# Sliding-window attention in a two-layer decoder kernel: queries and keys produced transposed and passed through DRAM, a query block's two score blocks merged into 128 columns, values as differences

## The chip, the cores and the metric

The kernel runs on one core of one Trainium2 chip. The metric is the device time of one execution in microseconds. Three runs before the change gave 2192.77 to 2192.95 us, median 2192.94.

The core's engines each work through an instruction queue of their own, in order: TensorE (PE in the profile; PEld is its weight load), VectorE (DVE), ScalarE (ACT), GpSimd (POOL), and SyncE (SP), which here only issues DMA transfers. They wait for each other through semaphores.

## The reference

Two layers on 1024 tokens of width 1024, batch 1. Layer 0 mixes tokens by a causal convolution module, layer 1 by sliding-window attention with 16 query heads of width 64, four groups of four heads, each group with one key and value head. After each mixer come a layer norm, a squared-ReLU MLP, another layer norm, and a gated embedding. The change concerns the attention of layer 1:

```python
q = partial_rope((x @ w_q).reshape(B, T, N_HEADS, HEAD_DIM), cos, sin)
scores = einsum("bnqkgd,bnskd->bnkgqs", q, kk) * HEAD_DIM ** -0.5
mask = (kpos >= 0) & (rel >= 0) & (rel < 128)          # rel = qpos - kpos
scores = where(mask, scores, -inf)
lse = logaddexp(logsumexp(scores, -1), sink)
out = einsum("bnkgqs,bnskd->bnqkgd", exp(scores - lse), vv)
return out.reshape(B, T, 1024) @ w_o
```

Queries come in 8 blocks n of 128 tokens; kk and vv hold for each the keys and values of the block before it and of its own, 256 positions s. A query at place a of its block sees the places s <= a of its own block and the places s > a of the block before: exactly 128 keys, one per place (block 0 sees its own only). RoPE turns the first 16 of a head's 64 dimensions.

## The kernel before

All matrices are float32, and each operand of a large product is split into a rounded high part and the rest (`split`, L533: a ScalarE cast and a VectorE subtraction; `prep`, L514, for weights). A product is then three matmuls (`mm3`, L537): high by high, high by low, low by high. One half of 512 output columns over 1024 inputs is 24 matmuls.

The program is recorded, then put in order by a scheduler (`Recorder.schedule`, L304) that keeps a cost for each operation (`cost`, L276) and writes out one fixed queue per engine; all instructions are issued from one line, L452, so the profile is read by tile names, not by lines. Tiles are slots of a tag (`SLOTS`, L51: "A" has 9, "t" 5, "z" 4, "ps" 6 banks of PSUM and so on); the requests for a tag are served in the order in which the program makes them (`serve`, L367), and `move` (L224) hands slots from one tag to another. `later` (L263) lowers the priority of what stands in it. `Stream` (L455) prepares weight units of 128x1024 in five slots ahead of use.

The order of stages is `conv`, `mlp(0)`, `ple(0)`, `attention`, `mlp(1)`, `ple(1)` (L1500 to L1506). `embed` (L853) multiplies the per-layer inputs by a projection and leaves the result in DRAM for `ple`; that of layer 1, 96 matmuls of 512 columns, stands at the end of `conv`, after layer 0's `mix_out` (L873).

In `attention` (L1307) before the change:

- For each of 8 token tiles, `tok_group` (L624) makes keys and values together: the tile's transposed input is the stationary operand, 512 weight columns move past it. `rope` (L1291) turns keys by five small operations; `split` and four TensorE transposes make them stand with dimensions on partitions, high and low part one over the other (`kT`, tag B).
- For each pair of groups `gp` and each block `n`, 24 matmuls make 512 query columns (eight heads), `rope` turns them, and GpSimd copies them doubled. Then for each of the two groups `scores` (L1397) and, one step behind, `values` (L1447) are called: 32 calls of each in all.
- `scores` transposes the queries of four heads (4 transposes), splits them, and makes two matmuls of 256 columns for each head. VectorE adds the mask, scales and takes the maximum in one operation per head; ScalarE takes the exponential of 257 columns (256 keys and the sink) and sums them in its accumulator; VectorE inverts the sum; GpSimd scales.
- `values` transposes the probabilities of four heads (4 transposes per key block, so 8), splits them, and makes 4 matmuls of 512 columns that add up in one bank; ScalarE and VectorE fold its two halves and split the result into the operand of w_o.
- `mix_out` multiplies by w_o in groups of tiles (`MIX_GROUPS`, L48): first half of the columns in two groups of four tiles, second half in four pairs, each tile followed by its layer norm.

## Time and profile before

| what | value |
|---|---|
| median of three runs | 2192.94 us |
| span of the profiled execution | 2191.9 us |
| TensorE granted clock, mean | 0.999 |
| TensorE instructions | 10395 matmuls and transposes |
| bytes moved by DMA | 303.92 MB |

In the rows of the profile an operation is named by its tiles, "written <- read", with the number of partitions and elements; "ident" as an operand marks a transpose. The attention's score banks show as "B,g", the probabilities' transposes as "ident,z", the values' products as "A,v" or "A,bo" (the tags that lent the slots). Busy time is the time in which an engine had an instruction under way; a matmul's length includes the time that its last columns need to leave the array, so back-to-back matmuls overlap in the record.

### The profile page before, as it was taken

Reading aid. Unit: us, or ns where it says so; the run is one execution under the profiler, and the core shown is the slowest. Engines: PE = TensorE matmul, PEld = TensorE weight load, DVE = VectorE, ACT = ScalarE, POOL = GpSimd, SP = SyncE. Lnnn points to the kernel's source line nnn. Section 1 sums busy time; section 2 is a strip of 40 time slices with the busy share of each in tenths; the row PEclk is TensorE's granted clock in tenths of the full one; section 3 lists DMA queues with packets and bytes.
Section 4 is the critical chain, followed back from the end, with each engine's and each line's share of the span. In section 5 each row is a group of like instructions: output and inputs, shape, how many; then the busy total and the mean of one; then the engine's idle time right before and its main releaser. Section 6 shows DMA issues by size and latency. Waiting matters only on the chain. (4 is left out here: it accounts for less than half of the span.)

```text
span 2191.9 us, 29197 instructions
## 1 busy us (share of the span) xinstructions
PE 2179.6 (99%) x10395; PEld 1813.9 (83%) x10395; DVE 1654.1 (75%) x2744; ACT 929.4 (42%) x1712; POOL 245.0 (11%) x442
## 2 busy tenths in 40 slices
PE   9999999999999999999999999999999999999999
PEld 7888878888888888888888888888888888888887
DVE  6667786967776988789644888689677689778983
ACT  4233343544443333343335878444344433333441
POOL 0000043200000000002201544240000000000040
PEclk9999999999999999999999999999999999999999
DMA  7443632534446845451431011322444496455312
GB/s 227 116 115 87 194 118 87 202 100 155 159 149 239 293 162 181 140 186 38 135 101 39 20 39 30 117 103 98 148 150 154 153 323 222 140 176 174 105 68 101
DMA packets 142914, 303.92 MB, mean 139 GB/s; under 512 B 15664, under 2 KB 43696, under 8 KB 142768
## 3 DMA queue, kind: packets, MB, share of 16 engines
q1 hardware_dynamic: 141472, 301.26, 41.9%
q8 instruction: 82, 1.34, 0.3%
q10 hardware_dynamic: 1296, 0.79, 0.1%
q14 instruction: 64, 0.52, 0.1%
HBM read 212.86 MB, written 89.13 MB: 138 GB/s over the span
## 5 line engine op out<-in xcount | busy, mean ns | idle before, releaser
L452 PE MATMUL ps<-xTh 128*128 128x512 f32 x636 | 247.4, 389 | 0.0
L452 PE MATMUL ps<-xTl,xTh 128*128 128x512 f32 x636 | 247.4, 389 | 0.0
L452 PE MATMUL ps<-xTh,xTl 128*128 128x512 f32 x636 | 247.4, 389 | 0.0
L452 PE MATMUL ps<-xTl,wh 128*128 128x512 f32 x628 | 246.6, 393 | 0.0
L452 PE MATMUL ps<-xTh,wh 128*128 128x512 f32 x628 | 245.0, 392 | 0.7 <-ACT xTh L452 0.7
L452 PE MATMUL ps<-xTh,wl 128*128 128x512 f32 x628 | 245.5, 391 | 0.0
L452 ACT CAST wh<-raw 128x1024 fp32r<-128x1024 f32 (+2 forms) x138 | 129.2, 938 | 242.3 <-PE ps L452 128.3
L452 DVE TENSOR_TENSOR wl<-raw,wh 128x1024 fp32r<-128x1024 f32 (+2 forms) x138 | 151.6, 1099 | 103.6 <-ACT wh L452 103.1
L452 PE MATMUL ps<-wh,xTh 128*128 128x512 f32 (+1 forms) x452 | 178.4, 395 | 0.3 <-ACT xTh L452 0.3
L452 PE MATMUL ps<-wl,xTh 128*128 128x512 f32 (+1 forms) x452 | 178.3, 394 | 0.0
L452 PE MATMUL ps<-wh,xTl 128*128 128x512 f32 (+1 forms) x452 | 178.2, 395 | 0.0
L452 PEld LDWEIGHTS ps<-xTh,wh 128*128 128x128 f32 x628 | 118.4, 189 | 26.2 <-ACT xTh L452 1.4
L452 PEld LDWEIGHTS ps<-xTh 128*128 128x128 f32 x636 | 119.4, 188 | 25.0
L452 PEld LDWEIGHTS ps<-xTl,xTh 128*128 128x128 f32 x636 | 119.4, 188 | 24.9
L452 PEld LDWEIGHTS ps<-xTh,xTl 128*128 128x128 f32 x636 | 119.4, 188 | 24.5
L452 PEld LDWEIGHTS ps<-xTh,wl 128*128 128x128 f32 x628 | 118.5, 189 | 24.5
L452 PEld LDWEIGHTS ps<-xTl,wh 128*128 128x128 f32 x628 | 118.5, 189 | 23.0 <-DVE xTl L452 0.2
L452 POOL TENSOR_SCALAR sm<-sm 128x1 f32<-128x1 f32 x40 | 14.6, 366 | 1056.5 <-DVE sm L452 1054.9
L452 ACT CAST xTh<-wh 128x1024 fp32r<-128x1024 f32 x74 | 77.6, 1049 | 121.9 <-PE ps L452 79.3
L452 DVE TENSOR_TENSOR wl<-g,wh 128x512 fp32r<-128x512 f32 x100 | 66.5, 687 | 81.2 <-ACT wh L452 81.2
L452 ACT CAST wh<-g 128x512 fp32r<-128x512 f32 x100 | 59.6, 620 | 159.6 <-PE ps L452 69.5
L452 DVE TENSOR_TENSOR E<-cst,g 128x1152 fp32r<-128x1152 f32 x64 | 86.1, 1353 | 43.4 <-PE ps L452 42.6
(305 smaller groups left out, 5178.2 us busy)
## 6 DMA issues: line engine op xcount, KB each, us to landing
wh<-hid SPq DMA_DIRECT2D x76, 512.0 KB, 4.2
raw<-in_w_up_dram SPq DMA_DIRECT2D x64, 512.0 KB, 3.6
wl<-in_w_down_dram SPq DMA_DIRECT2D x64, 512.0 KB, 4.6
hid<-zz SPq DMA_DIRECT2D x84, 256.0 KB, 2.9
hid<-t SPq DMA_DIRECT2D x78, 256.0 KB, 2.1
raw<-hid SPq DMA_DIRECT2D x34, 512.0 KB, 4.1
B<-scr SPq DMA_DIRECT2D x32, 256.0 KB, 4.2
t<-proj SPq DMA_DIRECT2D x32, 256.0 KB, 3.5
```

Of the source, the lines that this page charges most:

```text
L452: getattr(getattr(nc, o.eng), o.name)(*a, **k)
```

## The change

Weights of queries and keys become the stationary operand, so that the products come out with dimensions on partitions (`part_rows`); no query or key is transposed any more. The weight columns are put in order on the host so that one product of 128 rows holds the same four or eight dimensions of all heads (block 0 and 1: the two RoPE halves), and RoPE works on whole rows (`rope_queries`, `keep_keys`). High and low parts are stored to DRAM (`qd`, `kd`) and come back per block and group, gathered by head, high over low (`load_queries`, `load_keys`). The queries of the first two groups are finished before the first score, those of the other two between the halves (`rest(0)`, `rest(1)`). Values are made by a product of 256 columns per tile.

In `scores` the two key blocks' scores of a head (256 columns of a bank) are merged into 128: ScalarE copies the earlier block's, VectorE's `copy_predicated` writes the own block's over them where s <= a. Maximum and sum become `tensor_reduce` over 129 columns of four heads at once. In `values` the one merged block is transposed (4 transposes); the product uses the earlier block's values with all probabilities, and adds the difference of the two blocks' values (`load_values`) with those probabilities that belong to the own block, which GpSimd cuts out by `affine_select`. The first half's output goes through DRAM (`ad`), because its place in `xTh` and `xTl` still holds the input of `rest(1)`. Layer 1's `embed` moves from the end of `conv` to the end of the attention steps; `mix_out` of layer 1 works in pairs of tiles in both halves; tags A and B change places for layer 1's residual tiles. Of `attention`, `scores` and `values`, the diff below shows the lines after the change.

```diff
+PAIRS = ((0, 1), (2, 3), (4, 5), (6, 7))
 MIX_GROUPS = (
-    ((0, 1, 2, 3), (4, 5, 6, 7)), ((0, 1), (2, 3), (4, 5), (6, 7)),
+    (((0, 1, 2, 3), (4, 5, 6, 7)), PAIRS), (PAIRS, PAIRS),
...
-        with nc.later(EMBED_BY[1]):
-            self.embed(1, (0, 1), "t")
...
+    def part_rows(self, u, h):
+
+        wh, wl = u
+        ps = self.ps()
+        self.mm3(ps, [
+            (wh[:, kb * P : (kb + 1) * P], wl[:, kb * P : (kb + 1) * P], *self.xs(kb, h * HT, HT)) for kb in range(KB)
+        ])
+        return ps
...
+        nc.scalar.mul(h, src, HD ** -0.5)
+        nc.vector.scalar_tensor_tensor(
+            out=l, in0=src, scalar=HD ** -0.5, in1=h.bitcast(F32), op0=ALU.mult, op1=ALU.subtract
+        )
...
+    def keep_rows(self, what, pair, parts, row, first, step, h):
+
+        cols = slice(h * HT, (h + 1) * HT)
+        n = parts.stop - parts.start
+        for v, t in zip(what, pair):
+            dst = self.dram(
+                v, (row,), cols, lambda a: a[first : first + (n - 1) * step + 1 : step, cols], n
+            )
+            self.nc.sync.dma_start(dst, t.bitcast(F32)[parts])
...
+    def rope_queries(self, x1, x2, h):
+
+        nc = self.nc
+        cs, sn = (v[:, h * HT : (h + 1) * HT] for v in self.rt)
+        for k, (a, b, op) in enumerate(((x1, x2, ALU.subtract), (x2, x1, ALU.add))):
+            m, n = self.sb("t"), self.sb("t")
+            nc.vector.tensor_tensor(out=m, in0=a, in1=cs, op=ALU.mult)
+            nc.vector.tensor_tensor(out=n, in0=b, in1=sn, op=ALU.mult)
+            nc.either.tensor_tensor(out=m, in0=m, in1=n, op=op)
+            self.keep_query(m, k, 4 * k, 8, h)
...
+    def load_queries(self, n, g):
+
+        q = self.sb("X", F32R)
+        tk = slice(n * P, (n + 1) * P)
+        rows = (0, 1) + tuple(2 + 3 * (g // 2) + c for c in range(3))
+        for k, v in enumerate(self.qd):
+            src = self.dram(
+                v, rows, tk, lambda a: a.rearrange("(h r) t -> r h t", r=HD)[:, 4 * g : 4 * g + 4, tk], HD
+            )
+            dst = q.bitcast(F32)[k * HD : (k + 1) * HD].rearrange("p (h t) -> p h t", h=4)
+            self.nc.sync.dma_start(dst, src)
+        return q
...
+        self.split(src(n), v[:, :, 0, :], v[:, :, 1, :])
+        if n:
+            w = self.sb("t")[:, 0:P].rearrange("p (g e) -> p g e", g=2)
+            nc.either.tensor_tensor(out=w, in0=src(n), in1=src(n - 1), op=ALU.subtract)
+            self.split(w, d[:, :, 0, :], d[:, :, 1, :])
+        return v, d
...
+        for h in range(2):
+            ps = [self.part_rows(u, h) for u in us[2:]]
+            self.rope_queries(*ps, h)
+            for k in range(2):
+                self.keep_keys(k, self.part_rows(us[k], h), h)
+
+        def rest(s):
+            for c in range(1, 4):
+                u = ws.get(1)[0]
+                for h in range(2):
+                    self.keep_query(self.part_rows(u, h), 1 + 3 * s + c, s * HT + c, 4, h)
+                ws.done(1)
+
+        rest(0)
...
                 for gl in range(2):
+                    g = 2 * gp + gl
+                    p = self.scores(n, g, self.load_queries(n, g), keys[:, gl])
                     if pend:
                         self.values(*pend)
+                    pend = p, n, gl, gp, before, vd
+                before = vd
+            if gp == 0:
+                rest(1)
         self.values(*pend)
+        for a, b in moves:
             nc.move(b, a)
+        for q in range(4):
+            tk = slice(q * 256, (q + 1) * 256)
+            for x, v in zip((self.xTh, self.xTl), self.ad):
+                nc.sync.dma_start(x.bitcast(F32)[:, 0:4, tk], v.rearrange("p (k t) -> p k t", k=4)[:, :, tk])
+        self.embed(1, (0, 1), "t")
...
+        w = P if n == 0 else 2 * P
+        s = nc.tile("z", (P, 2 * ZC)).rearrange("p (a b) -> p a b", a=4)
+        nc.gpsimd.tensor_copy(s[:, :, P], self.sink[:, 4 * g : 4 * g + 4])
         for jj in range(2):
             ps = self.ps("sc").rearrange("p (a b) -> p a b", a=2)
             for j in range(2):
+                qs = q[:, (2 * jj + j) * P : (2 * jj + j + 1) * P]
+                nc.tensor.matmul(ps[:, j, 0:w], qs, keys[:, 0, 0:w], start=True, stop=False)
+                nc.tensor.matmul(ps[:, j, 0:w], qs, keys[:, 1, 0:w], start=False, stop=True)
+            dst = s[:, 2 * jj : 2 * jj + 2, 0:P]
+            if n == 0:
+                mask = self.mask.unsqueeze(1).to_broadcast([P, 2, P])
+                nc.vector.tensor_tensor(out=dst, in0=ps[:, :, 0:P], in1=mask, op=ALU.add)
+                continue
+            nc.scalar.copy(dst, ps[:, :, 0:P])
+            mine = self.mine.bitcast(mybir.dt.int32).unsqueeze(1).to_broadcast([P, 2, P])
+            nc.vector.copy_predicated(dst, mine, ps[:, :, P : 2 * P])
+        sm = self.small(16)
+        nm, su = (sm[:, 4 * i : 4 * i + 4] for i in range(2))
+        nc.vector.tensor_reduce(out=nm, in_=s[:, :, 0 : P + 1], axis=AXIS, op=ALU.max, negate=True)
         for h in range(4):
+            nc.scalar.activation(s[:, h, 0 : P + 1], s[:, h, 0 : P + 1], AF.Exp, bias=nm[:, h : h + 1], scale=1.0)
+        nc.vector.tensor_reduce(out=su, in_=s[:, :, 0 : P + 1], axis=AXIS, op=ALU.add)
         nc.vector.reciprocal(su, su)
         for h in range(4):
             nc.gpsimd.tensor_scalar(
+                out=s[:, h, 0:P], in0=s[:, h, 0:P], scalar1=su[:, h : h + 1], scalar2=0.0, op0=ALU.mult, op1=ALU.add
             )
+        return s
+
+    def values(self, s, n, gl, gp, before, vd):
         nc = self.nc
+        pp = self.transpose4([s[:, h, 0:P] for h in range(4)])
+        pT = [self.sb("A", F32R) for j in range(2)]
+        self.split(pp, *pT)
         po = self.ps("pv")
+
+        def v(x):
+            return x[:, gl].rearrange("p s e -> p (s e)")
+
+        tr = [(v((before or vd)[0]), p) for p in pT]
+        if n:
+            for p in pT:
+                m = self.sb("A", F32R)
+                nc.gpsimd.affine_select(
+                    out=m, in_=p, pattern=[[0, 4], [1, P]], compare_op=ALU.is_ge, fill=0.0, base=0, channel_multiplier=-1
+                )
+                tr.append((v(vd[1]), m))
         for i, (l, r) in enumerate(tr):
             nc.tensor.matmul(po, l, r, start=i == 0, stop=i == len(tr) - 1)
         pv = po.rearrange("p (a e t) -> p a e t", a=2, e=2)
             r = slice(e * HD, (e + 1) * HD)
             nc.scalar.copy(s[r], pv[0:HD, :, e, :])
             nc.vector.tensor_tensor(out=s[r], in0=s[r], in1=pv[HD:P, :, e, :], op=ALU.add)
+        g = 2 * gp + gl
+        tk = slice(n * P, (n + 1) * P)
+        if gp:
+            sl = (slice(None), slice(2 * g, 2 * g + 2), tk)
+            self.split(s, self.xTh[sl], self.xTl[sl])
+            return
+        w = self.sb("t", F32R)
+        pair = [w[:, k * 256 : (k + 1) * 256].rearrange("p (a t) -> p a t", a=2) for k in range(2)]
+        self.split(s, *pair)
+        for x, y in zip(self.ad, pair):
+            nc.sync.dma_start(x.rearrange("p (k t) -> p k t", k=4)[:, 2 * g : 2 * g + 2, tk], y.bitcast(F32))
```

More of the change, by code (lines that the diff above doesn't have):

```diff
@@ L14 @@
 ALU = mybir.AluOpType
+AXIS = mybir.AxisListType.X
 P = 128
@@ L55 @@
 LATE = 100
-EMBED_BY = (150, 0)
+EMBED_BY = 150
 MARK = (3, 3)
@@ L871, in embed, with mix_out @@
         ws.done(len(us))
-    def mix_out(self, i, w, gb, tiles, lhs=None):
+    def mix_out(self, i, w, gb, tiles):
         nc, ws = self.nc, self.ws
@@ new lines, in keep_rows, with keep_query @@
+    def keep_rows(self, what, pair, parts, row, first, step, h):
[6 more added lines that the diff above has]
+            self.nc.sync.dma_start(dst, t.bitcast(F32)[parts])
+    def keep_query(self, src, row, first, step, h):
+        pair = [self.sb("A", F32R) for k in range(2)]
+        self.scaled_split(src, *pair)
+        self.keep_rows(self.qd, pair, slice(0, P), row, first, step, h)
```

236 lines of the change are left out of this document (100 added, 136 removed).

## The prediction, made before the changed kernel was timed

> **What bounds the kernel now.** I read the page's header and part 1 first.
>
> ```profile
> span 2191.9 us, 29197 instructions
> PE 2179.6 (99%) x10395; PEld 1813.9 (83%) x10395; DVE 1654.1 (75%) x2744; ACT 929.4 (42%) x1712; POOL 245.0 (11%) x442
> ```
>
> TensorE is busy 99% of the span: work taken from it shortens the kernel as long as the rest keeps up. The windows view (length, busy time and count of PE, PEld, DVE, ACT, POOL, then granted clock, DMA share, GB/s) shows how near the others come in the stage that changes.
>
> ```profile
> 400.00:450.00 50.00, 50.00 (x225) 41.28 (x224) 49.44 (x76) 25.41 (x43) 0.29 (x1) 1.00 0.47 162
> 550.00:600.00 50.00, 50.00 (x222) 41.35 (x222) 38.34 (x59) 21.07 (x35) 0.00 (x0) 1.00 0.47 160
> 1129.90:1468.20 338.30, 337.71 (x1826) 279.97 (x1825) 243.04 (x718) 207.66 (x582) 116.66 (x254) 1.00 0.17 55
> 1200.00:1250.00 50.00, 49.93 (x303) 42.45 (x303) 41.09 (x144) 37.92 (x114) 22.43 (x60) 1.00 0.04 12
> 1250.00:1300.00 50.00, 50.00 (x291) 41.24 (x290) 44.93 (x151) 42.09 (x123) 25.55 (x61) 1.00 0.16 53
> 1400.00:1468.20 68.20, 68.20 (x320) 56.61 (x319) 44.57 (x62) 21.08 (x28) 19.44 (x21) 1.00 0.23 78
> ```
>
> Attention runs from 1129.9 (first key product) to 1468.2 (last w_o product). At 1250 TensorE is full, but VectorE is at 90% and ScalarE at 84%: the softmax steps are covered only because the query products, 12 matmuls per step, stand between them. A matmul's shown duration includes its pipeline, so I take the pace. The window at 550 holds only 512-column matmuls: 50/222 = 0.225 us each. The timeline (start, length, ...) gives the others:
>
> ```profile
> 246.74 2.56 PE L452 MATMUL ps<-B,E 128*128 128x256 f32 x20
> 1103.26 1.48 PE L452 MATMUL ps<-ident,E 128*128 128x128 f32 x12
> 1193.49 0.56 PE L452 MATMUL ps<-B,g 128*128 128x128 f32 x4
> ```
>
> Less one drain of 0.28: 0.120 us per 256-column matmul, 0.110 per transpose, 0.10 per 128-column matmul.
>
> **The change, part by part.** *TensorE.* From the order of both built programs: 400 transposes become 128 (272 x 0.110 = 29.9 us less); scores 192 of 256 columns and 96 of 128 become 224 and 32 (32.6 to 30.1 us, 2.5 less); keys and queries keep their columns, but values take 192 matmuls of 256 columns for 96 of 512 (23.0 for 21.6, 1.4 more); probabilities times values stay at 120 of 512. Sum: 31 us less work. The stage's 1826 instructions at these paces (1080 x 0.225, 192 x 0.120, 96 x 0.10, 458 transposes x 0.110) are 326 of its 338.3 us; the other 12 are small bubbles.
>
> *Where cover goes.* Now all queries of eight heads are made first, then 16 (block, group) steps follow, then the queries of the other eight heads, then 16 steps. TensorE's own work in 16 steps is 112 x 0.120 + 16 x 0.10 + 60 x 0.225 + 64 x 0.110 = 35.6 us, 2.2 a step. The order shows what is left to fill with. In the first 16 steps: 48 of the 144 matmuls of the second query half, nearly all in the first four steps; the rest, 94 in one run, comes when 15 steps are done. In the second: 46 of the 96 matmuls of the moved embedding (12 ahead, 34 among the last four steps), then 50 in one run, then w_o. Tile queues are served first come first, so the embedding's copies wait for the attention's "t" tiles, and w_o's banks for the embedding's. So the steps run at the pace of VectorE and ScalarE. Their prices, groups by form between 1180 and 1400 us (last pair: busy us, mean ns; idle behind the bar):
>
> ```profile
> L452 DVE TENSOR_TENSOR A<-ps,A 128x512 fp32r<-128x512 f32 x60 | 40.0, 686 | 5.0 <-ACT A L452 4.5
> L452 DVE TENSOR_TENSOR t<-t,ps 64x256 f32<-64x256 f32 x64 | 27.1, 424 | 7.4 <-ACT t L452 5.7
> L452 DVE CUSTOM_DVE_ANT_0 z<-ps,cst 128x256 f32<-128x256 f32 x56 | 22.8, 416 | 0.4
> L452 DVE CUSTOM_DVE_ANT_0 z<-ps,cst 128x128 f32<-128x128 f32 x8 | 2.2, 283 | 0.5 <-PE ps L452 0.3
> L452 DVE TENSOR_TENSOR xTl<-t,xTh 128x256 fp32r<-128x256 f32 x16 | 6.8, 422 | 0.6 <-ACT xTh L452 0.5
> L452 DVE RECIPROCAL sm<-sm 128x4 f32<-128x4 f32 x32 | 5.5, 172 | 4.4 <-ACT z L452 4.2
> L452 DVE TENSOR_TENSOR v<-A,v 128x128 fp32r<-128x128 f32 x5 | 1.5, 300 | 0.3 <-ACT v L452 0.3
> L452 DVE BATCH_NORM_STATS2 sm<-A 128x6 f32<-128x512 f32 x2 | 1.4, 686 | 0.0
> ...
> L452 ACT CAST A<-ps 128x512 fp32r<-128x512 f32 x60 | 33.2, 580 | 6.9 <-PE ps L452 6.9
> L452 ACT COPY t<-ps 64x256 f32<-64x256 f32 x64 | 23.3, 364 | 16.5 <-PE ps L452 9.2 <-DVE t L452 6.7
> L452 ACT CAST xTh<-t 128x256 fp32r<-128x256 f32 x16 | 6.4, 400 | 3.0 <-DVE t L452 3.0
> L452 ACT ACTIVATE z<-z,sm 128x129 f32<-128x129 f32 x16 | 6.3, 395 | 0.1
> ...
> L452 POOL COPY t<-t 128x512 f32<-128x512 f32 x32 | 20.7, 657 | 146.4 <-DVE t L452 129.5 <-issue 7.0 <-PE ps L452 4.5
> L452 POOL COPY z<-cst 128x2 f32<-128x2 f32 x60 | 15.0, 254 | 19.5 <-PE ps L452 18.2 <-PE tr L452 0.4 <-POOL z L452 0.2
> L452 POOL TENSOR_SCALAR z<-z,sm 128x128 f32<-128x128 f32 x16 | 5.7, 376 | 5.1 <-DVE sm L452 5.1
> L452 POOL TENSOR_TENSOR E<-z,g 128x512 f32<-128x512 f32 x11 | 17.8, 1628 | 12.1 <-DVE z L452 8.9 <-issue 3.2
> ```
>
> (The last row is from the whole trace.) VectorE in 16 steps: 32 masked copies or adds x 0.417 = 13.3; 32 reductions over 516 elements; 16 reciprocals 2.8; 16 splits of probabilities x 0.686 = 11.0; 32 adds x 0.424 = 13.6; 16 splits x 0.422 = 6.8; some 18 value operations x 0.30 = 5.4. A reduction isn't in the trace: from the 283 and 416 ns rows an element costs 1.04 ns, so 516 cost 0.54 us bare, and the statistics row, which reads 512 from the same memory, has 0.686; I take 0.68, that row, and keep 0.54. That is 21.8, and 75 us for 16 steps, 4.7 a step. The masked copy is bound by 0.283 (half its elements) and 0.686; it reads a bank as the 416 ns row does, so that.
>
> ScalarE: 64 exponentials x 0.395 = 25.3; 28 copies of 128x256, between 0.364 and 0.58, say 0.40, 11.2; 16 x 0.58, 32 x 0.364, 16 x 0.400 = 27.3; values 4.5: 68, and 3 to 5 for queries or embedding. GpSimd: 64 x 0.376 + 16 x 0.25 + four subtractions = 30, and 28 selections of 128x512, not in the trace: 0.657 (a copy of that shape) to 1.63 (a two-input operation), 48 to 75 us. I take 0.8, near the one-input row. On GpSimd's queue these selections stand between the scalings of the next steps, and TensorE's transposes wait for those.
>
> So 2 x 75 us of VectorE with ScalarE close behind. How full can it be? 99% at 400 us, 90% and 82% in attention before; I take 94.5%, between the first two, as here it isn't held by TensorE: 158.7 us. Each half also begins and ends with the chain through one step (a last step's split, selections and products follow VectorE's last reduction): 4 us in the first, where the run of 94 takes over early, 6 in the second. Both halves: 168.7.
>
> *Round trip.* Queries and keys go through DRAM: 220 more transfers on SP's queue (52 stores and 128 loads of queries and keys, 32 stores and 8 loads of attention output). At the start 23 us of value products hide it. Between the halves, the loads stand behind the last store on SP; that store waits for ScalarE's and VectorE's split.
>
> ```profile
> L452 SPq DMA_DIRECT2D raw<-in_w_q_dram x8: 327/332/333, 1120.3 to 1255.7; - x8
> ...
> t<-proj SPq DMA_DIRECT2D x32, 256.0 KB, 3.5
> ```
>
> 0.58 + 0.69 + two issues of 0.33 + a landing of 3.5 = 5.5 us from the last query matmul to the first score. Bounds: 0, if the 12 embedding matmuls and one step's values covered it, and twice that.
>
> *At nothing.* The embedding's 96 matmuls (21.6 us) move, and behind mix_out(0) the MLP's first products fill in, as they already do behind mix_out(1) at 1400-1468 (TensorE 68.20 of 68.20); uncovered, a normalisation's few us. Pairs in w_o's first half: weight preparation is off the path with VectorE idle there; uncovered, 2 us. RoPE on few rows, tag swaps: under the products.
>
> *Sum*, first key product to last w_o product: first products 336 x 0.225 + 23.0 + 34 leftover transposes 3.7 = 102.3; halves 168.7; 94 matmuls 21.1; round trip 5.5; 50 embedding matmuls 11.3; w_o 384 x 0.225 + 24 transposes = 89.0. Total 398; before 338.3 + 21.6 of embedding elsewhere = 359.9. **38 us more**: 31 us of TensorE work saved, some 80 of idle TensorE bought, 12 of bubbles traded. 2191.9 + 38 = 2230; the median of the runs shown, 2192.94, lies 1 us above the span: **2231**.
>
> Low end: 99% full, reductions at 0.54, half the chain ends: 2 x 70.5/0.99 + 5 = 147, 21 less: 2210. High end: 82% full: 183 + 10, 24 more: 2255.
>
> **Rivals.** (a) *The clock falls.* With 2.2 us of work in 5 TensorE may not count as busy.
>
> ```profile
> 251.62 0.47 PE L452 MATMUL ps<-wh,wh 128*128 128x512 f32 x1 [2.33 <-DVE g L452]
> ...
> 303.32 0.66 PE L452 MATMUL ps<-ident,A 128*128 128x128 f32 x4 [1.82 <-ACT t L452]
> ...
> 252.00:256.00 4.00, 4.00 (x13) 2.85 (x12) 3.02 (x5) 0.00 (x0) 0.21 (x1) 0.57 0.95 298
> ```
>
> After 2.33 us idle the granted clock fell to 0.57 of full over 4 us; after 1.82 us it didn't. A step has under 3 us idle, in several pieces, which speaks against. At half clock throughout, TensorE needs 2 x (35.6 + 48 x 0.225) = 92.8 and 2 x (35.6 + 34 x 0.225) = 86.5, and sets the pace: 179 + 10, 21 more: 2252. The Trainium skill (TensorE: Matmul & The Clock Gate, "What's actually happening") says that the clock halves after one idle window of about 3.4 us. By that rule alone the steps would keep full clock; the trace agrees in the half rate but shows that 2.33 us idle can do.
>
> (b) *GpSimd becomes the bound*, stretched as its operations are where VectorE contends: at 1.63 per selection and 0.6 per scaling (1.6 times its row) 16 steps are 90 us, /0.945 x 2 + 10 = 200, 32 more: 2263. Against: at 90% VectorE the 376 ns row held. The Trainium skill (GPSIMD Engine Reference, "Elementwise — side-by-side cycle accounting") puts data-dependent branching at about 12 cycles per element of a 1.2 GHz clock; as an estimate from that page a selection would take 5.1 us and the kernel some 190 us more. No run here shows it.
>
> (c) *Transfers bound the first half*: per step 260 KB of queries, 260 of keys, 260 of stores, in pieces of 512 B to 1 KB.
>
> ```profile
> 90.00:120.00 30.00, 30.00 (x167) 25.99 (x166) 19.18 (x29) 8.86 (x22) 0.81 (x6) 1.00 0.41 97
> ```
>
> With such pieces 97 GB/s took 0.41 of the engines, 237 GB/s full: 3.3 us a step, below 4.7. At half that rate 6.6 us, 106 + 4 for the half, 26 more: 2257.
>
> (d) *Not slower.* The halves would have to fit into 398 - 38 = 360, that is 131 us instead of 169: 60 us of VectorE for 16 steps at 99%. One mechanism can: the forms without an accumulator are cheap, reductions and masked copies at half price (75 - 17.5 = 57.5) and exponentials at 0.20 (68 - 12.5 = 56 on ScalarE): 2 x 57.5/0.99 + 10 = 126, 5 us faster: 2188. It decides from 3.7 us a step down. Against: these rows scale with elements.
>
> **How the numbers follow.** Forecast 0.62 (2231, own range 2210 to 2255); (a) 0.12; (b) 0.10; (c) 0.08; (d) 0.08. The range 2210 to 2263 leaves out (d) and a tenth of the rest. A measurement of this kernel can tell 0.2% (4.4 us) from no change: (d) splits into 0.06 faster and 0.02 the same; slower has 0.92.
>
> **What would show it.** Right: the changed profile has two stretches of some 83 us with VectorE over 85% busy, in which TensorE starts about half of what it could (drains raise its busy share), a run of query products between them with VectorE nearly idle, idle of PE ended by POOL, DVE and ACT tiles, and 272 transposes fewer. The reductions, masked copies and selections then have rows of their own. Wrong: TensorE above 90% through attention, a step under 4 us, or a stall outside attention.

## The result, and the profile after

The changed kernel takes 2252.2 us (median of 4 runs, 2249.9 to 2252.8) beside 2192.9 for the kernel before (4 runs): 1.027 of its time, 95% interval 1.025 to 1.028. The profiled execution has a span of 2250.3 us, 58.4 more than before. The direction and the range of the prediction held; its middle was 21 us too low.

The changed kernel's page: span, busy time of each engine, and two rows of the 40 slices.

```profile
span 2250.3 us, 28661 instructions
PE 2190.7 (97%) x10187; PEld 1804.0 (80%) x10187; DVE 1651.6 (73%) x2478; ACT 891.4 (40%) x1552; POOL 244.7 (11%) x431
...
PE   9999999999999999999999777999999999999999
...
PEclk9999999999999999999999879999999999999999
```

TensorE lost 208 instructions (272 transposes and 32 score matmuls less, 96 value matmuls more), and yet three slices now show it at 70 to 80% busy, where no slice of its row did before. Its total busy time even rose, by 11 us. Outside attention, where TensorE is full, it takes some 12 us longer (below). In attention its busy time fell by only 2 us (357.30, for 337.71 before and 21.6 of embedding), because shown durations are longer there at the lower clock: a score matmul of 256 columns shows 0.340 us between 1217 and 1416, before the change 0.284 and 0.307. Counts, not busy shares, tell the work here.

The windows view of the changed kernel cuts attention at its own boundaries: the whole stage; the first 16 steps and 35 us from their middle; the query products of the second half; the gap to its first score; the second 16 steps; w_o. Columns as in the prediction.

```profile
1114.10:1520.20 406.10, 357.30 (x1713) 289.57 (x1712) 243.33 (x459) 181.92 (x442) 115.89 (x245) 0.93 0.50 147
1217.80:1298.40 80.60, 63.21 (x296) 48.92 (x296) 69.53 (x156) 58.84 (x167) 44.81 (x109) 0.84 0.55 151
1245.00:1280.00 35.00, 25.78 (x118) 18.88 (x118) 31.70 (x73) 26.59 (x80) 22.29 (x54) 0.90 0.44 124
1298.40:1321.10 22.70, 22.70 (x95) 18.10 (x94) 4.87 (x8) 3.86 (x7) 0.00 (x0) 0.96 0.50 158
1321.10:1339.70 18.60, 4.22 (x20) 3.12 (x18) 5.39 (x11) 4.15 (x10) 1.46 (x3) 0.67 1.09 292
1339.70:1416.10 76.40, 60.21 (x286) 46.81 (x287) 65.92 (x151) 57.67 (x169) 45.35 (x109) 0.88 0.42 109
1428.50:1520.20 91.70, 91.70 (x420) 75.52 (x419) 52.17 (x71) 24.73 (x33) 19.44 (x21) 1.00 0.24 82
```

Attention took 406.1 us; before it took 338.3, and the embedding that has moved into it some 21.6 elsewhere: 46 us more. The first steps are as forecast in kind: in the middle of a half VectorE is at 91% (31.70 of 35) while TensorE starts 118 instructions in 35 us, 3.4 a us, where before it started 5.8 a us (x291 in 50). Only the first 21 us of the first half are different: there the query products that the order left among the first steps keep TensorE full (21.20 of 21.20 us up to 1239). Between the halves VectorE nearly idles (4.87 of 22.70). Then comes what was forecast at 5.5 us and took 18.6. The stage began at 1114.1, where 1129.9 - 21.6 = 1108.3 was due, and 730.1 us followed it, where 723.7 did before: another 12 us (5.8 + 6.4) lie outside attention.

The same kernel's waits of TensorE between 1327 and 1416 (total, times, longest), the chain to the first score from the split of the query product that block 0 waits for, the last for tokens 0 to 511 (start, length, what), and two rows of SyncE's queue in that stretch:

```profile
PE ps L454 <- DMA X<-qdl: 14.4, 1, 14.4
PE tr L454 <- DVE t L454: 5.2, 7, 1.4
PE ps L454 <- POOL z L454: 4.5, 5, 1.8
```

```profile
1315.79 0.61 ACT A L454
...
1316.41 8.75 DMA qdh<-A
...
1327.88 5.65 DMA X<-qdh
...
1333.55 6.12 DMA X<-qdl
...
1339.71 4.78 PE ps L454 x20
```

```profile
1325.23 5.41 SPq L454 DMA_DIRECT2D X<-qdh  x8
...
1333.55 6.32 SPq L454 DMA_DIRECT2D X<-qdl  x8
```

The store of the high parts took 8.75 us to land and the first two loads 5.65 and 6.12, under a DMA share of 1.09 (the row of 1321.10 above). The second load could not have gone out much earlier even if the first had landed sooner: on SyncE's queue the high parts of eight steps and four other transfers are issued ahead of the first low part, from 1325.23 to 1333.55, 8.3 us in all with no pause over 0.5 us. The DMA issues of that stretch (1300 to 1345; KB each, median us to landing) name what else was under way:

```profile
xTl<-adl SPq DMA_DIRECT2D x4, 512.0 KB, 8.1
xTh<-adh SPq DMA_DIRECT2D x4, 512.0 KB, 6.4
X<-qdh SPq DMA_DIRECT2D x10, 128.0 KB, 5.6
...
X<-qdl SPq DMA_DIRECT2D x8, 128.0 KB, 6.3
```

The reload of the first half's attention output is eight transfers of 512 KB, 4 MB in all. Six of them are issued between 1312.7 and 1318.9, each as soon as the last query products have read the place that it fills, and so they are under way together with the query stores and loads for which TensorE waits.

The prices that the prediction had to bound, from the changed kernel's groups by form between 1217 and 1416:

```profile
L454 ACT ACTIVATE z<-z,sm 128x129 f32<-128x129 f32 x128 | 47.7, 403 | 18.3 <-DVE sm L454 17.4
L454 POOL TENSOR_SCALAR z<-z,sm 128x128 f32<-128x128 f32 x128 | 47.5, 384 | 116.4 <-DVE sm L454 88.8 <-ACT z L454 27.2 <-ACT v L454 0.5
L454 DVE TENSOR_REDUCE sm<-z 128x4 f32<-128x516 f32 x64 | 43.5, 682 | 1.9 <-ACT z L454 0.8
L454 POOL TENSOR_SCALAR_AFFINE_SELECT A<-A 128x512 fp32r<-128x512 f32 x56 | 36.9, 660 | 11.4 <-ACT A L454 8.4 <-DVE A L454 2.4
...
L454 DVE COPY_PREDICATED z<-cst,ps 128x256 f32<-128x256 int32 x56 | 23.8, 440 | 3.2 <-ACT z L454 2.2
```

Reductions 0.682 (0.68 taken), masked copies 0.440 (0.417), exponentials 0.403 (0.395), selections 0.660 (0.8). GpSimd is busy 44.8 and 45.4 us of the two halves, less than VectorE and ScalarE. The 116.4 us of idle time in its first row are mostly not in the steps: one wait of 71.1 us stands ahead of the first scaling and one of 22.4 between the halves.

### The profile page after: what moved, and what is told of

It is laid out like the page before. It is cut to its first block, busy times and chain, and to the rows that moved or that the text cites. A ratio compares the mean times of both kernels' runs of the same rounds, so it can differ in the third digit from the quotient of the medians.

```text
span 2250.3 us, 28661 instructions
## 1 busy us (share of the span) xinstructions
PE 2190.7 (97%) x10187; PEld 1804.0 (80%) x10187; DVE 1651.6 (73%) x2478; ACT 891.4 (40%) x1552; POOL 244.7 (11%) x431
## 4 chain that ended last, share of the span: by engine, by line
PE 45%; DVE 5%; DMA 2%; ACT 1%; issue 1%; SPq 0%; POOL 0%; ACTq 0%; DVEq 0%
PE ps L454 29%; PE tr L454 15%; DVE sm L454 1%; DVE A L454 1%; DVE t L454 1%; DVE xTl L454 1%; ACT z L454 1%; DVE z L454 0%; DVE B L454 0%; DVE wl L454 0%; DMA qdh<-A 0%; DMA X<-qdl 0%; DMA proj<-t 0%; ACT t L454 0%; DMA X<-qdh 0%
## 5 line engine op out<-in xcount | busy, mean ns | idle before, releaser
L454 PE MATMUL ps<-xTl,wh 128*128 128x512 f32 x744 | 295.7, 398 | 0.0
L454 PE MATMUL ps<-xTh,wl 128*128 128x512 f32 x744 | 295.0, 397 | 0.0
L454 PE MATMUL ps<-xTh,wh 128*128 128x512 f32 x744 | 294.3, 397 | 0.1
L454 PE MATMUL ps<-xTl,xTh 128*128 128x512 f32 x618 | 240.4, 389 | 0.0
L454 PEld LDWEIGHTS ps<-xTh,wh 128*128 128x128 f32 x744 | 140.4, 189 | 32.9 <-ACT xTh L454 0.9
L454 PEld LDWEIGHTS ps<-xTh,wl 128*128 128x128 f32 x744 | 140.2, 188 | 32.4
L454 PEld LDWEIGHTS ps<-xTl,wh 128*128 128x128 f32 x744 | 140.1, 188 | 31.7 <-DVE xTl L454 0.2
L454 PE MATMUL ps<-wl,xTh 128*128 128x512 f32 (+1 forms) x392 | 150.5, 384 | 0.0
L454 PE MATMUL ps<-wh,xTh 128*128 128x512 f32 (+1 forms) x392 | 150.0, 383 | 0.3 <-ACT xTh L454 0.3
L454 PE MATMUL ps<-wh,xTl 128*128 128x512 f32 (+1 forms) x392 | 149.8, 383 | 0.0
```

The lines of the kernel that those rows point to most:

```text
L454: getattr(getattr(nc, o.eng), o.name)(*a, **k)
```

## The experiments

**Outside attention: a start address.** TensorE is full in the convolution and the MLP before and after, but over the same stretch (450 to 700) the changed kernel starts fewer instructions, first before, then after:

```profile
450.00:700.00 250.00, 250.00 (x1105) 206.77 (x1104) 170.35 (x261) 101.46 (x166) 0.21 (x1) 1.00 0.46 154
```

```profile
450.00:700.00 250.00, 250.00 (x1088) 203.68 (x1087) 179.78 (x274) 101.35 (x166) 0.00 (x0) 1.00 0.50 173
```

17 fewer at 0.226 us are 3.8 us in 250, at full clock, with no wait. The change cuts the constants' tile from (256 + 256 + 32) x 4 = 2176 to (256 + 16) x 4 = 1088 bytes a partition, so the tiles allocated behind it, xTh and xTl among them, start 1088 bytes earlier, which is 8.5 times 128. The timelines show where the pace is lost. In the changed kernel twenty matmuls in a row with xTh or xTl as their moving operand start 0.2335 us apart (487.36 to 492.03), in the kernel before 0.2265 (487.95 to 492.48). Those that stream tiles of the tags A and B keep 0.227 in both. Two runs move the address alone, one in each kernel:

```diff
# e1_align, in the changed kernel (two places)
-256 + NH
+256 + 2 * NH
# e2_shift, in the kernel before
-256 + NT * 32 + 2 * NH
+256 + NT * 32 + 3 * NH
```

> The changed kernel with 64 bytes more in the constants tile ahead of xTh and xTl, so that these start at a multiple of 128 bytes again, as they did before the change. Theory (the smaller constants tile moved xTh and xTl by half a line, and products that stream them run at 233 ns a matmul instead of 226.5): the matmuls with xTh or xTl as the moving operand go back to 226.5 ns, some 6 us come back in each MLP's first part and 3 to 4 in the attention's products, 2252 to about 2238. Rival (the slower pace comes from other transfers or engines at that time, or from the chip): pace and time stay, 2252.

> The kernel before, with 64 bytes more in its constants tile and nothing else: xTh and xTl move off the multiple of 128 bytes. Theory (start of the streamed operand): the kernel before slows by some 10 to 15 us, in the stages whose matmuls stream xTh and xTl, to about 2205. Rival (the shift does nothing): 2193.

e1_align: 2236.7 us (ratio 1.0202, 1.0185 to 1.0219), 15.5 less than the changed kernel. e2_shift: 2206.3 (1.0064, 1.0049 to 1.0079), 13 more than before. The same stretch of 250 us, and attention, in e1_align; then the stretch in e2_shift:

```profile
450.00:700.00 250.00, 250.00 (x1104) 206.80 (x1103) 181.54 (x276) 103.01 (x169) 0.00 (x0) 1.00 0.53 179
1107.60:1510.60 403.00, 353.53 (x1715) 290.52 (x1714) 242.76 (x458) 180.93 (x442) 116.44 (x245) 0.94 0.51 148
```

```profile
450.00:700.00 250.00, 250.00 (x1096) 205.32 (x1095) 170.75 (x261) 100.36 (x164) 0.21 (x1) 1.00 0.45 149
```

With 64 bytes more the count is back at 1104, attention starts at 1107.6 (1108.3 was due), and 2234.9 - 1510.6 = 724.3 us follow it (723.7 before). So all of the loss outside attention, and 3 us inside it, is the address. In e2_shift the matmuls that stream xTh and xTl start 0.2295 us apart (489.40 to 493.99). Moving the embedding did not slow the MLP's start by anything that this sum shows.

**Does VectorE pace the halves?** Three runs load or unload one engine each.

```diff
# e4_nomax: no maximum, no bias of the exponential
-        nc.vector.tensor_reduce(out=nm, in_=s[:, :, 0 : P + 1], axis=AXIS, op=ALU.max, negate=True)
...
-AF.Exp, bias=nm[:, h : h + 1], scale=1.0
+AF.Exp, scale=1.0
# e5_noselect: own block's differences times uncut probabilities
-                m = self.sb("A", F32R)
-                nc.gpsimd.affine_select(out=m, in_=p, ...)
-                tr.append((v(vd[1]), m))
+                tr.append((v(vd[1]), p))
# e8_twice: every product of values a second time
-        for i, (l, r) in enumerate(tr):
-            nc.tensor.matmul(po, l, r, start=i == 0, stop=i == len(tr) - 1)
+        for k in range(2):
+            for i, (l, r) in enumerate(tr):
+                nc.tensor.matmul(po, l, r, start=i == 0, stop=i == len(tr) - 1)
```

> The changed kernel without the maximum over a row: the reduction is left out and the exponential taken without a bias. That is 32 reductions of 0.68 us, 22 us of VectorE in both halves. Theory (VectorE sets the pace of the 16 steps): the halves of 80.7 and 76.5 us shrink by 8 to 11 us each, the kernel by 16 to 22. Rival (GpSimd, the clock or the chain through one step sets it): under 8 us in all; chain alone (0.7 us of 5 in the chain of a step with four steps under way): about 5.

> The changed kernel without the selections: the products of the own block's value difference take the whole probabilities, not those cut to the own block. 56 selections x 0.66 = 37 us leave GpSimd, and TensorE's last two products of a step no longer wait for them; nothing else changes. If VectorE paces the halves: each within 2 us of the changed kernel's (80.7 and 76.4), the kernel within 4 us of 2252. If GpSimd paces them, or the selections delay the scalings that TensorE waits for: 10 us or more faster, 2242 or below.

> The changed kernel with every product of probabilities and values made a second time into the same sum: 120 more matmuls of 512 columns, 60 x 0.225 = 13.5 us of TensorE work in each half, no work more for any other engine (the output becomes twice as large). If VectorE paces the halves, TensorE has the room: each half grows by 0 to 5 us, the kernel by 0 to 10 (2252 to 2262), and the granted clock in the halves rises. If TensorE paces them, at its lower clock or through its queue's order, each grows by 13 us or more: 2278 or above.

The two halves of e4_nomax in the windows view, then those of e5_noselect, then those of e8_twice:

```profile
1219.10:1292.10 73.00, 59.81 (x304) 46.59 (x303) 61.40 (x143) 53.13 (x167) 45.22 (x106) 0.93 0.63 166
...
1329.70:1400.80 71.10, 56.70 (x286) 45.94 (x287) 56.05 (x135) 52.68 (x169) 44.45 (x109) 0.89 0.47 119
```

```profile
1219.50:1295.90 76.40, 62.07 (x306) 46.64 (x305) 68.45 (x155) 58.19 (x167) 29.28 (x84) 0.93 0.58 162
...
1335.40:1413.70 78.30, 65.92 (x294) 49.54 (x295) 66.52 (x152) 59.78 (x172) 28.73 (x81) 0.88 0.48 130
```

```profile
1224.10:1309.40 85.30, 70.36 (x362) 56.99 (x361) 71.62 (x157) 58.46 (x167) 44.19 (x108) 0.94 0.51 145
...
1347.20:1427.80 80.60, 69.55 (x348) 55.37 (x349) 66.88 (x151) 59.60 (x172) 46.48 (x109) 0.95 0.43 112
```

27 us of TensorE work went in for 4.7 + 4.2 us of the halves and 5.6 us of the kernel (2257.8; 1.0291, 1.0275 to 1.0307), and the granted clock rose from 0.84 and 0.88 to 0.94 and 0.95. (The profiled run took 2262.8 us, 5 more than the median.) TensorE has room, and its lower clock is a sign of idleness, not the pace. e5_noselect took 37 us from GpSimd and gave 4.8 (2247.4; 1.0245, 1.0226 to 1.0264), a little more than the 4 allowed and half of what GpSimd as the bound would give. Its first half fell by 4.2 us, twice the 2 allowed, and its second grew by 1.9: in the first half the selections do cost something. e4_nomax took 32 x 0.682 = 21.8 us from VectorE and gave 14.7 (2237.5; 1.0205, 1.0184 to 1.0225), 7.6 of it in the first half and 5.3 in the second: two thirds, a little under what was expected, far above the rival's bound. VectorE sets most of the pace. What holds the steps once it is relieved was not tested: no run relieves ScalarE, busy 53 us of each half of e4_nomax, or shortens the chain through a step without unloading an engine.

**The gap between the halves.** e3_reload holds the reload of the attention output back until the second half has made its score products of block 3:

```diff
                     p = self.scores(n, g, self.load_queries(n, g), keys[:, gl])
+                    if g == 2 and n == 3:
+                        mark = [o for o in nc.ops if o.eng == "tensor"][-1]
...
             for x, v in zip((self.xTh, self.xTl), self.ad):
+              with nc.after(mark):
                 nc.sync.dma_start(x.bitcast(F32)[:, 0:4, tk], v.rearrange("p (k t) -> p k t", k=4)[:, :, tk])
```

> The changed kernel with the eight transfers that bring the first half's attention output back into xTh and xTl held until the sixth step group of the second half (behind the scores of block 3). Theory (the round trip of the last queries took 18.8 us instead of 5.5 because their store and loads shared the transfer engines with these 4 MB): the time from the last query matmul to the next score falls to 8 to 11 us and the kernel gains 8 to 10 us, 2243. Rival (the order of loads on SP's queue, high parts of eight steps ahead of the first low part, makes it long): 16 us or more remain, gain under 3 us.

Its gap and its second half:

```profile
1324.90:1331.20 6.30, 4.12 (x20) 3.11 (x19) 3.57 (x5) 3.45 (x8) 1.47 (x3) 0.98 0.72 223
1331.20:1413.90 82.70, 63.32 (x291) 49.65 (x292) 67.79 (x158) 59.89 (x172) 45.66 (x109) 0.86 0.64 164
```

The gap fell from 18.6 to 6.3 us: the reload was what made it long, and each link of the chain is shorter without it. In e3_reload the store of the high parts has landed 2.4 us after its issue (1320.14 to 1322.54, when the first load goes out), the first low part is issued 5.2 us behind the first high part, and the first score comes 3.4 us later (1331.21). So the rival, the order of loads on SyncE's queue, holds 5 us of this chain even here. That 6.3 is close to the prediction's 5.5 is partly luck: the prediction began the chain behind the last query matmul, but block 0 needs only the products of tokens 0 to 511, and its loads start 2.5 us before that last matmul ends. The second half grew from 76.4 to 82.7, with a DMA share of 0.64 for 0.42, and 6.4 us are left of the gain, where 8 to 10 had been expected (2245.9; 1.0243, 1.0228 to 1.0259). What slows that half was not settled: a fuller DMA goes with it here, but e9_spread below has 91.0 us at 0.49, with more work in it.

**The embedding's place.** e6_embed puts the second embedding back at the end of the convolution; e10_tagB leaves it behind the steps, but its results go to another set of tiles:

```diff
# e6_embed: at the end of conv, instead of behind the steps of attention
+        self.embed(1, (0, 1), "t")
...
-        self.embed(1, (0, 1), "t")
# e10_tagB
-        self.embed(1, (0, 1), "t")
+        self.embed(1, (0, 1), "B")
```

> The changed kernel with the second embedding back at the end of the convolution, where it was before. The MLP's start gets its cover back: -4 us. In the second half 46 of its 96 matmuls stood among steps that VectorE paces; if those were covered, taking them elsewhere costs their whole 46 x 0.225 = 10.3 us, so 2252 + 6 = 2258 (2254 to 2262). Rival, that TensorE's work or the embedding's copies on ScalarE and VectorE set the second half's pace: the half falls by 8 us or more and the kernel is at 2248 or below.

> The changed kernel with one letter changed: the second embedding's results go to tiles of tag B, which is free during attention, instead of tag t, which the attention's steps use. In the order as built, 82 of its 96 matmuls then stand between the last query product of the second half and its first score (12 before), and 14 embedding and 85 w_o matmuls among the steps of the second half (34 embedding matmuls before). If the place in the queue of t tiles is what kept the embedding, and w_o behind it, out of the second half: the round trip's wait of 14.4 us is filled, the tail of 50 matmuls (12.4 us) goes, w_o after the last values shrinks by about 85 x 0.225 = 19 us, the second half grows by 3 to 5: 2252 - 26 = 2226, between 2219 and 2234, the gain of moving the embedding back (20) without moving it. Rival, that the embedding's place as such costs: 2246 or above.

e6_embed: 2232.2 (1.0178, 1.0163 to 1.0194), 20 us less; 6 more had been expected, so the theory that the embedding was cheap cover fell. Its whole attention stage and its second half:

```profile
1141.50:1505.30 363.80, 327.92 (x1619) 266.11 (x1618) 238.06 (x454) 170.21 (x422) 117.17 (x245) 0.94 0.52 147
...
1365.10:1444.70 79.60, 73.75 (x365) 57.98 (x366) 70.85 (x159) 55.43 (x163) 45.72 (x109) 0.93 0.40 101
```

TensorE starts 365 instructions in the second half (286 in the changed kernel) in 79.6 us for 76.4, beside 70.85 us of VectorE for 65.92: 113 of w_o's products, those for the heads of the first half, now fill in, which in the changed kernel stood behind the embedding. e10_tagB shows why the embedding did not fill in itself. Its tiles of tag "t" are given out in order behind those of the steps; with tag "B", 82 of its 96 matmuls stand in the gap and 85 of w_o's among the steps. The gap and the second half of e10_tagB:

```profile
1324.40:1347.30 22.90, 20.55 (x91) 16.09 (x89) 6.62 (x12) 11.77 (x23) 1.46 (x3) 1.00 1.06 290
1347.30:1432.10 84.80, 73.00 (x351) 57.46 (x352) 73.23 (x160) 60.06 (x170) 46.62 (x107) 0.88 0.66 172
```

The gap is full of work now (20.55 of 22.90), and the kernel falls to 2235.7 (1.0186, 1.0169 to 1.0203), 16.5 us less for one letter. 26 had been expected: the second half grew by 8.4 us, not by 3 to 5 (in e3_reload it grew too, by 6.3), and the gap itself from 18.6 to 22.9.

**What is left, put back step by step.** e7_three joins the aligned start, the gated reload and the embedding's old place. e9_spread adds to it that the six query products of the second eight heads are asked for one by one, behind blocks 1 to 6 of the first half:

```diff
# e9_spread, on top of e7_three
                     self.keep_query(self.part_rows(u, h), 1 + 3 * s + c, s * HT + c, 4, h)
+                    yield
                 ws.done(1)
+            yield
-        rest(0)
+        for k in rest(0):
+            pass
+        more = rest(1)
...
                 before = vd
-            if gp == 0:
-                rest(1)
+                if gp == 0 and n:
+                    next(more)
```

> The changed kernel with the streams' start put back to a multiple of 128 bytes, the reload of the attention output gated until the second half has begun, and the second embedding back behind the convolution. If the three effects add: -15.5 (seen alone), -6.4 (seen alone) and the embedding's (+6, if it was free cover in the second half and costs 4 us at the MLP's start) give 2252 - 16 = 2236, between 2228 and 2242. All theories: still slower than before by 30 us or more, since the halves at VectorE's pace remain; if it comes within 15 us of before (below 2208), the halves aren't the main term.

> The version with the three repairs (streams' start, gated reload, embedding back), and with the query products of the second eight heads asked for one at a time, one behind each query block from the second on in the first half, instead of all behind its last step. TensorE's work in the first half becomes 35.6 + 144 x 0.225 = 68 us, still under VectorE's 80, which gets some 6 splits more (about 5 us). If TensorE idles in the halves because VectorE paces them and nothing stands between, the run of 94 (22 us) and most of the round trip (6) vanish and the first half grows by 3 to 9 us: 2212.6 - 20 = 2193, between 2186 and 2202. Rival, that the steps' own chain is slowed by every product put between them as much as the run cost: within 6 us of 2212.

e7_three: 2212.6 (1.0086, 1.0072 to 1.0100), 24 below the expected 2236 because the embedding's sign was wrong there too; 15.5 + 6.4 + 20 = 42 us seen alone, 39.6 together. It is 19.4 us above the kernel before, where 30 or more had been forecast. e9_spread: 2192.6 (0.9995, 0.9986 to 1.0004), as expected, and not to be told from the kernel before. From its first score to the first score of the second half, and the second half; then the second half of e7_three:

```profile
1230.70:1311.80 81.10, 71.24 (x378) 57.15 (x376) 68.53 (x147) 57.05 (x157) 40.92 (x96) 0.97 0.70 202
...
1311.80:1402.80 91.00, 81.18 (x389) 63.50 (x390) 81.76 (x186) 64.14 (x191) 53.51 (x126) 0.88 0.49 139
```

```profile
1337.40:1421.00 83.60, 76.51 (x368) 61.43 (x369) 73.37 (x166) 56.39 (x165) 45.75 (x108) 0.88 0.55 152
```

Steps, query products and gap together take 81.1 us, where the changed kernel needed 80.6 + 22.7 + 18.6 = 121.9. Not all of that is gain: the values of the last steps have slid into the second half, which is 7.4 us longer than that of e7_three and has 8.4 us more of VectorE's work. From the first score to the last values it is 172.1 us (1230.7 to 1402.8) against 191.7 in e7_three (1229.3 to 1421.0), 19.6 less. The run of query products and the gap that it took away were some 28 us there (22 + 6), so about 20 of the 28 were free cover.

**The merge by itself.** h_merge is the kernel before, queries made per block among the steps as there, with merged scores and value differences alone (its `scores` and `values` are those of the change, with queries transposed per block). h_accum also takes the sum of the exponentials from ScalarE again:

```diff
# h_accum, on top of h_merge
-            nc.scalar.activation(s[:, h, 0 : P + 1], s[:, h, 0 : P + 1], AF.Exp, bias=nm[:, h : h + 1], scale=1.0)
-        nc.vector.tensor_reduce(out=su, in_=s[:, :, 0 : P + 1], axis=AXIS, op=ALU.add)
+            nc.scalar.activation(
+                s[:, h, 0 : P + 1], s[:, h, 0 : P + 1], AF.Exp, bias=nm[:, h : h + 1], scale=1.0,
+                accum_out=su[:, h : h + 1],
+            )
```

> The kernel before with two parts of the change alone: the two score blocks of a query block merged into 128 columns, and the value differences with their selections. The queries are made per query block as before, so 12 query matmuls still stand between the steps. TensorE loses 112 transposes (112 x 0.110 = 12.3 us); VectorE per step gets two reductions of 0.68 and two masked copies of 0.44 for four masked reductions of 0.416 and one split of 0.686 less, so about the same. If the loss of the change lies in taking the query products out of the steps, this version is faster than before by 6 to 13 us: 2180 to 2187. Rival, that the new forms on VectorE and the selections on GpSimd cost by themselves: slower than before by 5 us or more, above 2198.

> The kernel before with the merged scores and the value differences, and with the sum of the exponentials accumulated by ScalarE's exponential, as the kernel before does it, instead of by a reduction on VectorE. 32 reductions of 0.685 us leave VectorE (22 us of its 248 in attention), which was 93% busy in the windows of that version while TensorE fell to 94% in two of four; ScalarE has 69% to 77%. If VectorE's pace is what kept the 15 us of saved TensorE work from showing in full, attention falls from 331.9 to 318 to 326: 2174 to 2182. Rival, that the round of waits from score to transpose holds TensorE: within 3 us of 2188; or that the accumulating form costs ScalarE as much: 2186 or above.

h_merge: 2187.7 (0.9975, 0.9965 to 0.9986), faster than both kernels, by 5.5 us where 6 to 13 had been expected: just short of it. Two windows of its steps:

```profile
1190.00:1240.00 50.00, 50.00 (x293) 42.39 (x292) 42.87 (x107) 35.74 (x95) 27.50 (x63) 1.00 0.02 6
1240.00:1290.00 50.00, 46.76 (x264) 37.82 (x263) 46.53 (x108) 38.16 (x101) 31.24 (x64) 1.00 0.19 59
```

In the second VectorE reaches 93% and TensorE falls to 94%. The next two windows do not make this a rule: from 1290 TensorE is full with VectorE at 91%, from 1340 it is at 94% (46.83) with VectorE at 84%. h_accum: 2185.8 (0.9962, 0.9950 to 0.9975), which the intervals do not set apart from h_merge; 2174 to 2182 had been expected. Two of its groups in attention:

```profile
L453 ACT ACTIVATION_READ_ACCUMULATOR z<-z,sm 128x1 f32 x128 | 24.2, 189 | 0.0
...
L453 DVE TENSOR_REDUCE sm<-z 128x4 f32<-128x516 f32 x32 | 21.9, 685 | 0.3
```

The accumulator is read by an instruction of its own: 24.2 us came to ScalarE by this row for the 22 that left VectorE; the busy time of the two in attention went from 193.1 to 202.9 and from 247.8 to 233.0. TensorE's shown idle time there was small before (331.90 us less 325.15) and after (328.90 less 324.46), so there was little to win. Which of the two rivals holds, ScalarE's new load or the round of waits, these runs do not tell.

## Why the prediction was right or wrong

- *Right: cover, not work, decides.* The two stretches paced by VectorE with TensorE half used, the run of products between them and the fewer transposes are all there, and e4_nomax, e5_noselect and e8_twice name VectorE as the main pacer. e9_spread confirms it from the other side.
- *The halves: mechanism right, 11.7 us too long* (157.0 for 168.7), by two errors of opposite sign. VectorE was busy 69.5 and 65.9 us in them, not 75: some 3 us a half are value operations and small items that were fewer, the rest comes from adding shown durations end to end. The groups of the second half (1339.7 to 1416.1) add up to 71.8 us and were 65.9 of busy time, for the records of back-to-back VectorE instructions overlap by some 0.07 us. In the timeline of the changed kernel (start, length, what) each of these begins before the one ahead of it has ended:

```profile
1259.30 0.28 DVE L454 TENSOR_TENSOR bo<-t,bo 128x128 fp32r<-128x128 f32 x1
1259.50 0.16 DVE L454 RECIPROCAL sm<-sm 128x4 f32<-128x4 f32 x1
1259.59 0.74 DVE L454 COPY_PREDICATED z<-cst,ps 128x256 f32<-128x256 int32 x2
```

  And a half is filled to 86% by it (69.53 of 80.60, 65.92 of 76.40), ends included, not to 94.5%; the 91% in its middle is nearer. VectorE's prices for reductions, masked copies, adds and splits of probabilities, and ScalarE's for the exponential, were right within 6%. The selection was 0.660 for 0.8, ScalarE's copy of 128x256 0.364 for 0.40, and VectorE's split of 128x256 0.476 for 0.422.
- *The round trip: the step that failed inside attention*, 18.6 us for 5.5, outside its bounds of 0 and 11. The store and loads were costed by one landing of an idle moment, 3.5 us, and two issues of 0.33. That the reload of the attention output becomes free to go while the last query products run was not seen, nor that twelve issues, 8.3 us of SyncE's queue, stand ahead of the first low part. e3_reload without the reload: 6.3, by a chain that starts earlier than the prediction's.
- *The other parts*: products to the first score 103.7 (102.3), query run 22.7 (21.1), tail from the last values to w_o 12.4 (11.3), w_o 91.7 (89.0). In all attention is 8 us above its 398; 3 of these are the start address. That it came so close is partly luck: 11.7 us too much for the halves stand against 13.1 too little for the round trip.
- *"At nothing"*: the embedding's departure from the convolution cost next to nothing there: attention starts 19.7 us later in e7_three, which has it back (1127.3), than in e1_align (1107.6), for 21.6 us of work. Its tail in the new place was priced well, at 11.3 us where 12.4 came. What the sum does not show is that the new place was dear: by its terms, taking the embedding back to the convolution costs 21.6 - 11.3 = 10 us, and e6_embed, which does so, is 20 us faster, because w_o's products then fill the second half. The prediction said that w_o's banks wait for the embedding's, and drew no price from it.
- *Not in the sum at all*: 15.5 us of start address (12 outside attention, 3 inside), the larger part of the 21 by which the forecast was low. The prediction's own condition, a stall outside attention, caught it in kind, though it is a slower pace and not a stall.
- *Rivals.* (b) GpSimd is not the bound: 0.660 per selection, and 4.8 us from taking all of them away. (c) Transfers did not bound the first half, in which TensorE waited 0.3 us for one; they bound the gap behind it. (d) No form was cheaper than its row. (a) The clock did fall, to 0.84 and 0.88 in the halves, but e8_twice shows that it does not set their length; the time came to this rival's 2252 by other causes.

TensorE's longest kind of wait in the changed kernel's first half (total, times, longest), and the windows at that half's end, show how little idleness this took:

```profile
PE tr L454 <- DVE t L454: 8.3, 8, 2.1
```

```profile
1288.00:1295.00 7.00, 4.68 (x14) 3.02 (x12) 4.76 (x12) 5.06 (x14) 3.94 (x8) 0.50 0.44 141
1295.00:1299.00 4.00, 3.54 (x9) 2.80 (x10) 2.30 (x5) 0.97 (x3) 1.41 (x4) 0.50 0.74 250
```

The granted clock was 0.50 there, although no wait of that half was longer than 2.1 us and the five from 1280.6 to 1295.5 were of 0.6 to 1.5 us. By the Trainium skill (TensorE: Matmul & The Clock Gate, "What's actually happening") it takes one idle window of about 3.4 us. The trace shows the half clock after gaps that are all far shorter, one after the other, and the measurement decides.

## What to carry to other kernels

Work on a full engine is worth removing only as long as what stood beside it keeps its cover: here, with everything else repaired, query products in runs of their own left the kernel 20 us slower in spite of 31 us of saved TensorE work, and 144 of their 384 matmuls, asked for a piece at a time, took these 20 us back. When a block of independent work is put at the end of a stage, look at whose tiles and banks it queues for and what then queues behind it: one tile tag was worth 16 us. When a constant changes size, check that what is allocated behind it keeps the start it had.

## What the runs showed of the hardware that was not expected

- *The start address of a moving operand.* With xTh and xTl shifted by an odd multiple of 64 bytes against their start in the kernel before, the matmuls that stream them started 0.2335 us apart (changed kernel) or 0.2295 (e2_shift) for 0.2265, at full clock and without a wait. Over a mix in which only some read them as the moving operand that is 1088 or 1096 instructions in 250 us for 1104 or 1105, and the kernel lost 15.5 or 13 us. In two kernels the shift costs and in two its absence does not; the runs tell that the period is over 64 bytes and, if there is one, no more than 1024 (the shift of e1_align against before), not more. Why e2_shift, at the same offset modulo 128, lost only half as much per matmul was not settled, nor why tiles of other tags were streamed at the old pace, or whether these moved too.
- *A mask by selection on GpSimd is cheap*: 0.660 us for 128x512, against 0.657 for a copy of that shape (the prediction's row). The Trainium skill's accounting of data-dependent branching (GPSIMD Engine Reference, "Elementwise — side-by-side cycle accounting"), from which the prediction worked out an estimate of 5.1 us, does not apply to this instruction.
- *ScalarE's accumulating form* has a second instruction of 0.189 us, half of the exponential of 129 columns that it follows.
